# Attention: odd heads' softmax rows transposed into the two banks of other transposes, 13 steps behind the scores with a fourth row buffer

## The chip, the cores and the metric

The kernel runs on one core of a Trainium2 chip. The metric is device time in microseconds (us), the median of the runs shown. A profile records one execution: TensorE is PE in its rows (PEld for its weight loads), VectorE is DVE, ScalarE ACT, GpSimd POOL, and SyncE, which issues most transfers, SP. [...]

## The reference

Two layers of an encoder over 256 tokens of width 1024. Each layer is a half-step feed-forward block, two attention branches that share one projection, and another half-step feed-forward block:

```
x = x + 0.5 * swiglu(rms_norm(x, ffn1_norm), ...)
z = rms_norm(x, mix_norm) @ w_in          # na q|k|v, sw q, sw k|v, two gates
o_na = neighbourhood_attention(qa, ka, va, na_rpb)     # 8 heads of 64
o_sw = sliding_window_gqa(qs, ks_, vs, t5_bias, sink)  # 8 heads of 64, 2 key heads
merged = g[0] * (o_na @ w_branch_na) + g[1] * (o_sw @ w_branch_sw)
x = x + merged @ w_out
x = x + 0.5 * swiglu(rms_norm(x, ffn2_norm), ...)
```

Queries and keys are normalized for each head; scores get a bias (a learned one by relative position), and the sliding-window branch has a sink logit in its softmax. All is 32-bit floating point.

## The kernel before

**Precision.** Every large product is three products of halves. A value is split into a high and a low part (`split_to`, L181: ScalarE copies the high part, L182, and VectorE subtracts it, L183), and `three` (L167) issues high x high (L168), high x low (L169) and low x high (L170). A step below is one such triple of 128 x 512 matmuls.

**Order.** TensorE's order is that in which the code issues. A counter `now` advances by one with each step (`tick`), and `defer(lag, key, fn)` puts a piece of work into a list that `tick` empties when its time has come; `need(key)` calls it at once where its result is wanted. So the lags, counted in steps, say where in the stream of projection steps a piece of attention stands. The orders of ScalarE, VectorE, GpSimd and SP are laid out by a scheduler from the same program when it is built; each engine then takes its own queue in order.

**Attention.** `mix` runs the projection (w_in, in 512-column pieces), and between its steps the 16 heads, first the eight of the sliding-window branch (sw), then the eight of the neighbourhood branch (na). One head goes through these stages (`attend`, L520):

- `front` (L533): four score matmuls into a bank of tag sc (L547), bias and row maximum on VectorE into a row buffer S (L550), exponentials and sums on ScalarE (L553), the reciprocal on VectorE (L559), and the scaling of the rows on GpSimd (L560). S has LAG = 3 buffers.
- `turn` (L564), P_LAG = 10 steps later: four transposes of S into the one bank of tag pt (L568); ScalarE copies the high part ph out of it, and VectorE computes the low part pl, which reads pt too. Until pl is done the bank is taken.
- `back` (L575), V_LAG = 7.5 steps after that: four matmuls with v into po (L582), which ScalarE and VectorE combine into o (L586, L587); after every second head o is split into oB (sw) or oA (na).

**Other users of PSUM.** Projections and gates use two banks of tag g. Two banks of tag tp take the transposes of queries (L491) and keys (L508), of the merged branches (L707), of the normalized input (L199) and of the feed-forward block (L314). The low part of the keys, kl (L511), reads them, and the values va are read out of the g banks (L517, L518).

**Merge.** Behind the projection, `local` multiplies oB and `grid` oA with the branch weights. `grid` takes eight steps into banks br: k = 0, 1, 2 for both halves of the tokens, then k = 3 for both. The step k uses heads 2k and 2k + 1 of na, so k = 3 needs oA of heads 6 and 7. Weight pieces pass through a ring: a load into raw (4 buffers), ScalarE's wh and VectorE's wl (6 buffers each). The piece behind the branch weights is the first of w_out.

## Time and profile before

| what | value |
|---|---|
| median of 3 runs | 1088.5 us (1087.56 to 1088.72) |
| the profiled execution's own time | 1088.83 us |
| its span, first to last instruction | 1087.1 us |
| TensorE / VectorE / ScalarE / GpSimd busy | 1075.3 / 854.8 / 659.3 / 116.4 us |
| DMA: moved, mean rate | 212.63 MB, 196 GB/s |
| the attention stages | about 205 to 345 and 742 to 882 us |

A row of the timeline has its start, its length, the engine, the line, the operation with output and inputs, and in brackets how long the engine sat idle before it and what released it. Matmuls are pipelined, so one row's length reaches into the next; the distance of starts says how fast TensorE advances. A wait with several conditions is put down to the one that came last by the profile.

### The profile page before, as it was taken

How to read it: one execution, taken by the hardware profiler on the slowest of the kernel's cores; microseconds unless marked ns; L12 is line 12 of the kernel's file. 1: busy time of each engine (PE TensorE's matmuls, PEld its weight loads, DVE VectorE, ACT ScalarE, POOL GpSimd, SP SyncE). 2: the span in 40 equal slices, each digit the busy share in tenths (PEclk: the TensorE clock that was granted, in tenths of full speed). 3: DMA queues.
4: the chain of work that ended last, by engine and by line, in shares of the span. 5: the costliest groups of instructions: out<-in, count | busy, mean ns of one | idle time of the engine just before them, and what ended most of it. 6: DMA issues, size and time to landing. Idle time of an engine off the chain costs nothing.

```text
span 1087.1 us, 14699 instructions
## 1 busy us (share of the span) xinstructions
PE 1075.3 (99%) x5137; PEld 891.5 (82%) x5137; DVE 854.8 (79%) x1298; ACT 659.3 (61%) x1002; POOL 116.4 (11%) x118
## 2 busy tenths in 40 slices
PE   9999999999999999999999999999999999999998
PEld 6888888888888888888878888888888888888887
DVE  6888788889886778778877777888888767878785
ACT  6665654788764556565465656457877645656542
POOL 1400000243510000000000000003534000000000
PEclk9999999999999999999999999999999999999999
DMA  7876665755654676666657766547566555776652
GB/s 243 265 218 211 196 200 174 238 186 151 193 179 136 199 227 207 210 203 203 194 174 222 223 211 204 177 155 241 178 188 187 171 169 162 222 241 196 211 167 94
DMA packets 98828, 212.63 MB, mean 196 GB/s; under 512 B 7569, under 2 KB 13745, under 8 KB 98753
## 3 DMA queue, kind: packets, MB, share of 16 engines
q1 hardware_dynamic: 98560, 211.60, 62.3%
q8 instruction: 40, 0.66, 0.2%
q14 instruction: 36, 0.29, 0.1%
q0 software_dynamic: 192, 0.08, 0.1%
HBM read 210.59 MB, written 1.06 MB: 195 GB/s over the span
## 4 chain that ended last, share of the span: by engine, by line
PE 85%; DVE 8%; ACT 3%; issue 3%; DMA 1%; POOL 0%; ACTq 0%; DVEq 0%
PE g L168 19%; PE g L170 19%; PE g L169 18%; PE acc L168 6%; PE acc L170 6%; PE acc L169 6%; DVE wl L183 3%; PE tp L314 2%; ACT wh L182 1%; PE tp L169 1%; PE tp L170 1%; PE tp L168 1%; DMA raw<-in_w_d 1%; PE pt L568 1%; PE sc L547 1%
## 5 line engine op out<-in xcount | busy, mean ns | idle before, releaser
L183 DVE TENSOR_TENSOR wl<-raw,wh 128x1024 fp32r<-128x1024 f32 (+1 forms) x340 | 408.0, 1215 | 75.6 <-ACT wh L182 74.5
L182 ACT ACTIVATE wh<-raw 128x1024 fp32r<-128x1024 f32 (+1 forms) x340 | 348.8, 1044 | 117.4 <-PE g L170 39.3
L168 PE MATMUL g<-wh,xh 128*128 128x512 f32 (+1 forms) x976 | 386.1, 396 | 0.0
L170 PE MATMUL g<-wh,xl 128*128 128x512 f32 (+1 forms) x976 | 378.2, 387 | 0.7 <-DVE xl L183 0.7
L169 PE MATMUL g<-wl,xh 128*128 128x512 f32 (+1 forms) x976 | 377.9, 387 | 0.8 <-DVE wl L183 0.8
L170 PEld LDWEIGHTS g<-wh,xl 128*128 128x128 f32 x976 | 183.4, 188 | 40.8 <-DVE xl L183 2.1
L169 PEld LDWEIGHTS g<-wl,xh 128*128 128x128 f32 x976 | 183.9, 188 | 33.8 <-DVE wl L183 1.6
L168 PEld LDWEIGHTS g<-wh,xh 128*128 128x128 f32 x976 | 183.6, 188 | 32.5 <-DVE hh L445 0.2
L443 ACT ACTIVATE sg<-g,rs_y 128x256 f32<-128x256 f32 x88 | 41.2, 468 | 102.9 <-PE g L170 102.6
L342 DVE TENSOR_TENSOR u<-raw 128x512 f32<-128x512 f32 x56 | 38.5, 690 | 64.5 <-DMA raw<-in_w_d 64.1
L168 PE MATMUL acc<-wh,hi 128*128 128x512 f32 x200 | 78.9, 394 | 0.0
L170 PE MATMUL acc<-wh,lo 128*128 128x512 f32 x200 | 77.9, 390 | 0.0
L169 PE MATMUL acc<-wl,hi 128*128 128x512 f32 x200 | 77.9, 390 | 0.0
L174 POOL TENSOR_TENSOR rs_y<-ms,mhalf 128x1 f32<-128x1 f32 x12 | 6.6, 554 | 657.3 <-DVE ms L220 648.9
L445 DVE SCALAR_TENSOR_TENSOR hh<-g,rs_y,sg 128x256 f32<-128x256 f32 x88 | 42.2, 479 | 28.8 <-ACT sg L443 28.8
L182 ACT ACTIVATE corner<-raw 128x512 fp32r<-128x512 f32 x28 | 17.6, 629 | 62.3 <-DMA raw<-in_w_d 47.0
L560 POOL TENSOR_TENSOR S<-S,sm 128x512 f32<-128x512 f32 x32 | 37.1, 1159 | 71.5 <-DVE sm L559 45.4
L170 PEld LDWEIGHTS acc<-wh,lo 128*128 128x128 f32 x200 | 37.6, 188 | 8.0
L168 PEld LDWEIGHTS acc<-wh,hi 128*128 128x128 f32 x200 | 37.6, 188 | 7.5
L169 PEld LDWEIGHTS acc<-wl,hi 128*128 128x128 f32 x200 | 37.6, 188 | 7.5
L553 ACT ACTIVATE S<-S,mx 128x256 f32<-128x256 f32 x64 | 31.8, 498 | 7.5 <-DVE mx L550 7.4
L174 POOL TENSOR_TENSOR rs_y<-hv,mhalf 128x8 f32<-128x8 f32 (+1 forms) x16 | 27.0, 1693 | 31.4 <-DVE hv L476 28.4
(190 smaller groups left out, 1462.9 us busy)
## 6 DMA issues: line engine op xcount, KB each, us to landing
raw<-in_w_gu SPq DMA_DIRECT2D x176, 512.0 KB, 4.4
raw<-in_w_d SPq DMA_DIRECT2D x100, 512.0 KB, 4.4
raw<-in_w_in SPq DMA_DIRECT2D x64, 512.0 KB, 4.5
raw<-in_w_out SPq DMA_DIRECT2D x16, 512.0 KB, 3.5
bb<-in_b_gate SPq DMA_DIRECT2D x16, 256.0 KB, 3.4
raw<-in_w_bsw SPq DMA_DIRECT2D x8, 512.0 KB, 3.7
raw<-in_w_bna SPq DMA_DIRECT2D x8, 512.0 KB, 3.6
raw<-in_w_d SPq DMA_DIRECT2D x12, 256.0 KB, 2.6
```

Source lines behind the costliest of these rows:

```text
L168: nc.tensor.matmul(ps, xh, wh, start=first, stop=False)
L169: nc.tensor.matmul(ps, xh, wl, start=False, stop=False)
L170: nc.tensor.matmul(ps, xl, wh, start=False, stop=last)
L174: rstd_done[0] = nc.gpsimd.tensor_tensor(y, v, mhalf[:, :n], ALU.pow)
L182: linked("act", lambda: nc.scalar.activation(hi, src, AF.Copy))
L183: linked("dve", lambda: nc.vector.tensor_tensor(lo, src, hi.bitcast(F32), ALU.subtract))
L314: nc.tensor.transpose(tp[:, SLOT[t][i], :], hh[t][:, i * P:(i + 1) * P], ident)
L342: sub = lambda to, x, y: nc.vector.tensor_tensor(to, x, y, ALU.subtract)
L443: nc.scalar.activation(sg, ps[:, :FC], AF.Silu, scale=rstd[t])
L445: nc.vector.scalar_tensor_tensor(hh, ps[:, FC:], rstd[t], sg, op0=ALU.mult, op1=ALU.mult)
L553: nc.scalar.activation(S_[:, t, :], S_[:, t, :], AF.Exp, bias=mx[:, t:t + 1], scale=-1.0, accum_out=sm[:, t:t + 1])
L560: nc.gpsimd.tensor_tensor(S_, S_, sm.unsqueeze(2).to_broadcast([P, T, S]), ALU.mult)
```

## The change

Three edits. `turn` takes a bank of tag tp, of which there are two, for odd heads; of the sw branch (where sink_l is set) only from head 3 on. Even heads, and head 1 of sw, still use the one pt bank. P_LAG goes from 10 to 13, so each turn, and `back` behind it, stands three steps later in TensorE's order. LAG goes from 3 to 4, a fourth buffer S.

```diff
-LAG = 3
-H_LAG, NORM_LAG, QK_LAG, P_LAG, V_LAG, M_LAG = 7.9, 4.0, 16, 10, 7.5, 5.5
+LAG = 4
+H_LAG, NORM_LAG, QK_LAG, P_LAG, V_LAG, M_LAG = 7.9, 4.0, 16, 13, 7.5, 5.5
@@
                 @urgent
                 def turn(h, S_):
-                    tp = ps_acc.tile([P, T, T, P], F32, name="pt", tag="pt")
+                    if h % 2 and (sink_l is None or h > 1):
+                        tp = ps_tp.tile([P, T, T, P], F32, name="pt", tag="tp")
+                    else:
+                        tp = ps_acc.tile([P, T, T, P], F32, name="pt", tag="pt")
```

The lines behind it in the file are numbered three higher in the changed kernel (L568 becomes L571, L582 L585, L587 L590, L693 L696). Three places in the first layer follow; the second layer reads alike. The numbers in the names are those of buffers, and the brackets name the engines for whose signals an instruction waits.

TensorE at the transposes of na head 4, before:

```order
L582 MATMUL po_3156<-ph_3071,va_1815 128x256 [waits Activation_49]
L582 MATMUL po_3156<-pl_3072,va_1815 128x256
L582 MATMUL po_3156<-ph_3071,va_1815 128x256
L582 MATMUL po_3156<-pl_3072,va_1815 128x256
L568 MATMUL pt_3164<-ident_85,S_3039 128x128 [waits DVE_49,PE_49,Pool_49]
L568 MATMUL pt_3164<-ident_85,S_3039 128x128 x3
```

The same place in the changed program:

```order
L585 MATMUL po_3179<-ph_3099,va_1815 128x256 [waits DVE_49,Activation_49]
L585 MATMUL po_3179<-pl_3100,va_1815 128x256 [waits DVE_49]
L585 MATMUL po_3179<-ph_3099,va_1815 128x256
L585 MATMUL po_3179<-pl_3100,va_1815 128x256
L571 MATMUL pt_3187<-ident_85,S_3039 128x128 [waits PE_49,Pool_49]
L571 MATMUL pt_3187<-ident_85,S_3039 128x128 x3
```

The product ahead of it is now that of head 2, not of head 1, and the transposes no longer wait for VectorE.

TensorE in the merge, from behind the products of na head 7 (po, whose four rows stand directly ahead of this piece) to the seventh br step, before:

```order
L168 MATMUL br_3363<-wh_3352,oA_1817 128x512
L169 MATMUL br_3363<-wl_3353,oA_1817 128x512
L170 MATMUL br_3363<-wh_3352,oA_1817 128x512
L168 MATMUL br_3363<-wh_3352,oA_1817 128x512
L169 MATMUL br_3363<-wl_3353,oA_1817 128x512
L170 MATMUL br_3363<-wh_3352,oA_1817 128x512
L168 MATMUL br_3363<-wh_3358,oA_1817 128x512
L169 MATMUL br_3363<-wl_3359,oA_1817 128x512
L170 MATMUL br_3363<-wh_3358,oA_1817 128x512
L168 MATMUL br_3362<-wh_3358,oA_1817 128x512 [waits Activation_49]
L169 MATMUL br_3362<-wl_3359,oA_1817 128x512
L170 MATMUL br_3362<-wh_3358,oA_1817 128x512 [waits DVE_49]
```

And now, from the sixth br step to the seventh, with the products of na head 7 between them:

```order
L168 MATMUL br_3355<-wh_3350,oA_1817 128x512
L169 MATMUL br_3355<-wl_3351,oA_1817 128x512
L170 MATMUL br_3355<-wh_3350,oA_1817 128x512
L585 MATMUL po_3359<-ph_3331,va_1815 128x256 [waits DVE_49]
L585 MATMUL po_3359<-pl_3332,va_1815 128x256
L585 MATMUL po_3359<-ph_3331,va_1815 128x256
L585 MATMUL po_3359<-pl_3332,va_1815 128x256
L168 MATMUL br_3354<-wh_3350,oA_1817 128x512 [waits Activation_49]
L169 MATMUL br_3354<-wl_3351,oA_1817 128x512
L170 MATMUL br_3354<-wh_3350,oA_1817 128x512 [waits DVE_49]
```

The products of head 7 moved behind the three br steps that followed them, so that the step that reads their result (k = 3, first half of the tokens) stands right behind them.

VectorE in the same place, before (wl_3499 is the low part of the first w_out piece; the two rows o are those of na heads 6 and 7):

```order
L587 TENSOR_TENSOR o_3336<-o_3336,po_3335 64x256 [waits Activation_49]
L693 SCALAR_TENSOR_TENSOR gate1_1819<-gate1_1819,g_3328 128x512 [waits PE_49]
L183 TENSOR_TENSOR wl_3463<-raw_3460,wh_3462 128x1024 [waits DMAHW7_49,Activation_49]
L587 TENSOR_TENSOR o_3336<-o_3336,po_3335 64x256 [waits Activation_49]
L183 TENSOR_TENSOR oA_1817<-o_3336,oA_1817 128x256 [waits Activation_49]
L183 TENSOR_TENSOR wl_3499<-raw_3496,wh_3498 128x1024 [waits DMAHW0_49,Activation_49]
```

And now:

```order
L696 SCALAR_TENSOR_TENSOR gate1_1819<-gate1_1819,g_3319 128x512 [waits PE_49]
L183 TENSOR_TENSOR wl_3463<-raw_3460,wh_3462 128x1024 [waits DMAHW7_49,Activation_49]
L590 TENSOR_TENSOR o_3360<-o_3360,po_3359 64x256 [waits Activation_49]
L183 TENSOR_TENSOR wl_3499<-raw_3496,wh_3498 128x1024 [waits DMAHW0_49,Activation_49]
L590 TENSOR_TENSOR o_3360<-o_3360,po_3359 64x256 [waits Activation_49]
L183 TENSOR_TENSOR oA_1817<-o_3360,oA_1817 128x256 [waits Activation_49]
```

The low part of the w_out piece moved ahead of head 7's o. On ScalarE its high part moved likewise, ahead of that head's o.

## The prediction

> **What bounds the kernel now.** The page's busy table and its row of granted clock come first.

> ```profile
> PE 1075.3 (99%) x5137; PEld 891.5 (82%) x5137; DVE 854.8 (79%) x1298; ACT 659.3 (61%) x1002; POOL 116.4 (11%) x118
> PEclk9999999999999999999999999999999999999999
> ```

> TensorE is busy for 1075.3 of 1087.1 us at full clock, in an order fixed by hand. The change neither adds nor removes a matmul, so only TensorE's waits can change. I therefore read the busy time of the two attention stages (one for each layer), and of the two stretches in which TensorE waits longest there. Columns: stretch, length, PE, PEld, DVE, ACT and POOL busy (instructions), clock, DMA share, GB/s.

> ```profile
> 205.00:345.00 140.00, 137.82 (x753) 117.05 (x751) 117.61 (x230) 102.00 (x202) 45.59 (x37) 1.00 0.61 185
> 742.00:882.00 140.00, 137.85 (x752) 117.04 (x751) 117.87 (x230) 102.14 (x202) 45.32 (x37) 1.00 0.62 186
> 245.00:262.00 17.00, 16.14 (x91) 13.56 (x91) 15.96 (x37) 13.57 (x32) 7.26 (x7) 1.00 0.62 172
> 278.00:304.00 26.00, 24.96 (x137) 21.11 (x136) 22.65 (x47) 20.02 (x44) 12.50 (x10) 1.00 0.60 176
> ```

> TensorE idles 2.18 us in the first stage and 2.15 us in the second: no more than some 4.3 us can be won. VectorE is nearly full (15.96 of 17 us) where TensorE waits. The timeline, TensorE and VectorE, shows both waits of layer 0 and their twins:

> ```profile
> 259.05 0.39 PE L170 MATMUL g<-wh,xl 128*128 128x512 f32 x1
> 260.30 0.63 PE L568 MATMUL pt<-ident,S 128*128 128x128 f32 x4 [0.86 <-DVE pl L183]
> 301.87 0.28 PE L582 MATMUL po<-pl,va 128*128 128x256 f32 x1
> 303.18 0.63 PE L568 MATMUL pt<-ident,S 128*128 128x128 f32 x4 [1.03 <-DVE sm L559]
> 797.77 0.63 PE L568 MATMUL pt<-ident,S 128*128 128x128 f32 x4 [0.85 <-DVE pl L183]
> 840.61 0.63 PE L568 MATMUL pt<-ident,S 128*128 128x128 f32 x4 [1.01 <-DVE sm L559]
> 259.47 0.68 DVE L183 TENSOR_TENSOR pl<-pt,ph 128x512 fp32r<-128x512 f32 x1
> 302.36 0.68 DVE L183 TENSOR_TENSOR pl<-pt,ph 128x512 fp32r<-128x512 f32 x1
> 256.31 0.61 ACT L182 ACTIVATE ph<-pt 128x512 fp32r<-128x512 f32 x1
> ```

> Counted by these transposes, 260.30 is head 4 of the sliding-window branch (sw) and 303.18 head 4 of the neighbourhood branch (na). Both start right after the previous head's pl: 259.47 + 0.68 = 260.15, then 0.15 to the start; 302.36 + 0.68 = 303.04, then 0.14. So the wait is for the single pt bank, also where the row names another VectorE instruction that ended last (sm). The copy ph was done at 256.92, so pl itself stood 2.55 us in VectorE's queue.

> **The two waits go.** Both are even heads that wait for an odd one. With odd heads in the tp banks, head 4 shares its bank with head 2, a whole head earlier. The matmuls that read the late pl come later: in the new order po of sw 3 stands eight projection steps behind pt of head 3, and so does po of na 3: over 8 x 0.69 = 5.5 us, where pl ended 260.15 - 255.14 = 5.0 us behind its pt before (the pt row stands in the next part). Each wait's worth is start to start less the undisturbed spacing. The rows of the last term below give that spacing: 0.12 us after a 256-column matmul (324.74 to 324.86), and three steps of three 512-column matmuls in 2.06 us (324.86 to 326.92), so 0.69 for a step and 0.23 for a matmul. Thus 260.30 - 259.05 - 0.23 = 1.02 and 303.18 - 301.87 - 0.12 = 1.19, so 2.2 us for a layer, **4.4 us** for two (the idle times alone, 0.86 + 1.03 + 0.85 + 1.01, give 3.75: the lower bound).

> **What the moved steps do at the front.** Every pt stands three steps (2.1 us) later behind its scores. What VectorE has queued is the same work with two 0.4 us instructions (o and oB) fewer ahead of the second half of v:

> ```profile
> 255.14 0.60 PE L568 MATMUL pt<-ident,S 128*128 128x128 f32 x4
> 256.61 1.40 DVE L511 SCALAR_TENSOR_TENSOR kl<-tp,qkg,kh 128x512 fp32r<-128x512 f32 x2
> 257.93 0.41 DVE L183 TENSOR_TENSOR oB<-o,oB 128x256 fp32r<-128x256 f32 x1
> 259.07 0.48 DVE L518 SCALAR_TENSOR_TENSOR va<-g,rs_y,va 128x256 fp32r<-128x256 f32 x1
> 261.46 0.39 PE L168 MATMUL g<-wh,xh 128*128 128x512 f32 x1
> 250.73 1.99 DVE L183 TENSOR_TENSOR wl<-raw,wh 128x1024 fp32r<-128x1024 f32 x1
> ```

> That va releases the projection bank into which the matmul at 261.46 writes. Only pt of head 4 and one step lie between 260.30 and it, so this pt takes 261.46 - 260.30 - 0.69 = 0.47; in the new order it stands behind. Without it and without the wait the matmul comes at 261.46 - 1.02 - 0.47 = 260.0; va ends at 259.55 - 0.8 = 258.8: slack 1.2 us. Odd head 3 newly needs the tp bank of the last key transposes, which the first half of kl releases. In the new order pl of head 2 (0.60) and an o (0.4) stand behind kl instead of ahead: about 257.3 - 1.0 = 256.3, against pt of head 3 at 255.14 + 3 x 0.69 + 4 x 0.12 for one score group = 257.7. I take both at nothing; VectorE's doubled times (1.99 us, against 1.2 elsewhere, with GpSimd at work) can eat most of that, so their upper end is the whole present backlog less the slack, 2.55 - 1.2 = 1.4 us for a layer. A loss below nothing is excluded, as these are waits. Behind them TensorE's whole queue would stand.

> Of SP's queue, one b_gate load in each layer moves behind one more weight load. This is its row in the page's table of DMA issues, with the time to landing last:

> ```profile
> bb<-in_b_gate SPq DMA_DIRECT2D x16, 256.0 KB, 3.4
> ```

> A gate's projection ends eight steps (8 x 0.69 = 5.5 us) after that of the gate before, which frees the buffer; with 3.4 us for the load 2 us are left. I take nothing; if that cover were gone, a gate's bank would come free late, as in rival 3. GpSimd scales the same rows in the same order and gains 2.1 us; a fourth row buffer only lets scores start, and no score matmul waited for a row.

> **What becomes late next: the last head.** Three steps later there means into the merge. Its consumer does not move: the seventh of eight br steps (k = 3), which reads oA of na heads 6 and 7. Before, po of head 7 stood three br steps ahead of it; now it stands directly ahead. These are the rows of before:

> ```profile
> 324.74 0.28 PE L582 MATMUL po<-pl,va 128*128 128x256 f32 x1
> 324.86 0.40 PE L168 MATMUL br<-wh,oA 128*128 128x512 f32 x1
> 325.06 0.38 ACT L586 ACTIVATE o<-po 64x256 f32<-64x256 f32 x1 [1.47 <-DVE wl L183]
> 325.46 0.42 DVE L587 TENSOR_TENSOR o<-o,po 64x256 f32<-64x256 f32 x1 [0.42 <-ACT o L586]
> 325.92 0.42 ACT L182 ACTIVATE oA<-o 128x256 fp32r<-128x256 f32 x1 [0.49 <-DVE o L587]
> 326.37 0.43 DVE L183 TENSOR_TENSOR oA<-o,oA 128x256 fp32r<-128x256 f32 x1 [0.48 <-ACT oA L182]
> 321.76 1.23 DVE L183 TENSOR_TENSOR wl<-raw,wh 128x1024 fp32r<-128x1024 f32 x1 [0.85 <-ACT wh L182]
> 322.90 0.41 DVE L587 TENSOR_TENSOR o<-o,po 64x256 f32<-64x256 f32 x1
> 326.02 0.39 PE L170 MATMUL br<-wh,oA 128*128 128x512 f32 x1
> 326.49 1.06 ACT L182 ACTIVATE wh<-raw 128x1024 fp32r<-128x1024 f32 x1 [0.15 <-PE br L170]
> 326.92 0.39 PE L168 MATMUL br<-wh,oA 128*128 128x512 f32 x1
> 327.59 1.23 DVE L183 TENSOR_TENSOR wl<-raw,wh 128x1024 fp32r<-128x1024 f32 x1 [0.79 <-ACT wh L182]
> ```

> From the last po to the end of oA's high part: 325.92 + 0.42 - 324.74 = 1.60 us. At 326.92 it had been ready for 0.58 us: no wait. In the new order, with s the start of the sixth br step, the last of four po starts at s + 0.69 + 3 x 0.12 = s + 1.05 and the seventh step would start at s + 1.16. Its weight load would start one matmul (0.23) ahead, at s + 0.93. oA would be ready at s + 1.05 + 1.60 = s + 2.65.

> But the first w_out piece now stands ahead of this chain on ScalarE and VectorE (wh and wl were behind it). Its wh waits for the fifth br step, whose last matmul starts at s - 0.23: by 326.49 - 326.02 = 0.47 it starts at s + 0.24 and ends at s + 1.30, early enough for ScalarE's o at s + 1.37. Its wl starts 1.10 later than wh, at s + 1.34, and holds VectorE for 1.14 (the wl at 321.76 and the o behind it at 322.90); so VectorE's o starts at s + 2.48 instead of s + 1.77. Then 325.92 - 325.46 = 0.46 to ScalarE's oA, and 0.42: s + 3.36.

> What such a wait costs TensorE, layer 1's first projection shows, which waits for a stationary operand:

> ```profile
> 553.15 0.39 PE L169 MATMUL g<-wl,xh 128*128 128x512 f32 x1
> 553.46 0.68 DVE L183 TENSOR_TENSOR xl<-xg,xh 128x512 fp32r<-128x512 f32 x1
> 554.20 0.50 PE L170 MATMUL g<-wh,xl 128*128 128x512 f32 x1 [0.66 <-DVE xl L183]
> 554.53 0.39 PE L168 MATMUL g<-wh,xh 128*128 128x512 f32 x1
> ```

> Undisturbed, 554.53 would have been 553.15 + 0.46 = 553.61: lost 0.92. A weight load normally starts with the matmul ahead of its own, here at about 553.16; xl ended at 554.14, 0.98 later. So the loss is the lateness less 0.06: 3.36 - 0.93 - 0.06 = 2.37 us; with some 0.05 for oA's low part, 2.4 us for a layer, **4.8 us** for two. Bounds: 1.66 if that wl did not delay the chain (2.65 - 0.93 - 0.06), 2.5 if both low parts come late. No later work takes it up, as TensorE never idles behind it in the rows of before.

> **Sum.** -4.4 + 4.8 = +0.4 us. The profiled execution took 1088.83 (span 1087.1 and 1.73 around it), so 1089.2; the median of the runs is 0.33 lower, 1088.5, so **1088.9**. Bounds of the terms: -4.4 + 3.3 = -1.1 to -3.75 + 5.0 = +1.25, or 1087.4 to 1089.8.

> **Rivals.** (1) Forecast, a new wait as long as those removed: 0.64. (2) The chain from the last po costs TensorE less than its parts: faster from a wait under 1.1 us for a layer, down to 1084.1 without any. For it speaks that no br step waits now; against it, that four dependent instructions of 0.4 us follow po itself: 0.11. (3) Slower: the full VectorE queue at the front turns into a new wait for va's bank or kl's, from the point where va ends more than 1.2 us later than worked out. At 1.4 us for a layer that gives 1088.9 + 2.8 = 1091.7. For it: 15.96 of 17 us busy; against, less work ahead: 0.16. (4) The waits don't go (po then waits for the same pl): 1088.9 + 4.4 = 1093.3; against it speaks the distance worked out above: 0.06. (5) TensorE's clock falls after the long wait: 0.03. At the start of the program five matmuls take from 1.66 to 3.96:

> ```profile
> 1.66 2.50 PE L118 MATMUL idle<-blank 128*128 128x512 f32 x5 [1.66 <-DVE blank L113]
> 3.96 1.05 PE L199 MATMUL tp<-ident,x 128*128 128x128 f32 x4
> ```

> That is 0.46 each, twice the 0.23 above, though the clock row shows full speed. A slow stretch as long as these two rows (1.66 to 5.01) behind each wait would cost half its length, 1.7 us for a layer: 1092.3. Against it: after waits of 1.0 to 1.2 us the matmuls keep their pace. [...]

> **How the numbers follow.** What a measurement of this kernel can tell from no change is about 0.2%, 2.2 us. (2) is faster: 0.11. (1) is within it: 0.64. (3), (4) and (5) are slower: 0.25 together. The range reaches from the forecast's lower bound, with 0.6 us for what the walk leaves out, 1086.8, to (3) at 1092.0.

> **What would show it.** Right: no row of pt with an idle of 0.8 us or more; the seventh br step (L168) or its weight load waiting about 2.4 us for ScalarE's oA, in both layers, with a wl between ScalarE's and VectorE's o. Wrong: that wait under 1.6 us, or missing; a wait at a projection's first matmul or at a pt for kl; a clock under 1.0 behind the merge.

## The result: slower, with two waits that the prediction did not have

The changed kernel takes 1098.6 us (median of 4 runs, 1096.92 to 1099.25), against 1088.6 us (1087.56 to 1089.89) for the kernel before on the same chip: a ratio of 1.0087, 95% interval 1.0071 to 1.0103. It is slower by 10 us, where 1088.9 was forecast and 1092.0 was the upper end of the range. The profiled execution took 1099.25 us, its span 1097.5. Two executions of kernels below (1122.8 and 1805.6 us) ran throughout at a lower clock, 0.93 and 0.56 in the mean, and are left out of their medians and ratios.

First the page's busy row of the changed kernel:

```profile
PE 1080.3 (98%) x5137; PEld 894.6 (82%) x5137; DVE 860.8 (78%) x1298; ACT 658.3 (60%) x1002; POOL 119.8 (11%) x118
```

Then the view of its waits on TensorE (engine, output and line, releaser; us in total, times, the longest):

```profile
PE po L585 <- DVE o L590: 5.5, 4, 1.6
PE br L168 <- ACT oA L182: 4.3, 2, 2.2
```

Two things are to be seen. The waits of pt have gone from the list, as predicted, and br waits for oA, as predicted. But po waits for o, four times and for longer in all, and that stands nowhere in the prediction. And TensorE is busy for 5 us more with the same 5137 matmuls, so some of them were slow. The timeline has the new waits, each with the row ahead of it (TensorE, both layers):

```profile
268.95 0.39 PE L170 MATMUL g<-wh,xl 128*128 128x512 f32 x1
270.71 0.39 PE L585 MATMUL po<-ph,sv 128*128 128x256 f32 x1 [1.37 <-DVE o L590]
...
316.14 0.40 PE L170 MATMUL g<-wh,oB 128*128 128x512 f32 x1
318.09 0.39 PE L585 MATMUL po<-ph,va 128*128 128x256 f32 x1 [1.55 <-DVE o L590]
...
328.19 0.28 PE L585 MATMUL po<-pl,va 128*128 128x256 f32 x1
330.63 0.50 PE L168 MATMUL br<-wh,oA 128*128 128x512 f32 x1 [2.17 <-ACT oA L182]
...
811.76 0.39 PE L170 MATMUL g<-wh,xl 128*128 128x512 f32 x1
813.15 0.38 PE L585 MATMUL po<-ph,sv 128*128 128x256 f32 x1 [1.00 <-DVE o L590]
...
858.59 0.40 PE L170 MATMUL g<-wh,oB 128*128 128x512 f32 x1
860.54 0.39 PE L585 MATMUL po<-ph,va 128*128 128x256 f32 x1 [1.56 <-DVE o L590]
...
870.67 0.28 PE L585 MATMUL po<-pl,va 128*128 128x256 f32 x1
873.11 0.50 PE L168 MATMUL br<-wh,oA 128*128 128x512 f32 x1 [2.16 <-ACT oA L182]
```

Start to start, less the undisturbed 0.23 or 0.12 us, po lost 1.53, 1.72, 1.16 and 1.72 (6.1 us), and br 2.32 twice (4.6 us). Counted by their places, the po are those of sw head 4 and na head 5.

Behind the wait for oA the matmuls change their pace:

```profile
330.97 0.50 PE L169 MATMUL br<-wl,oA 128*128 128x512 f32 x1
331.27 0.63 PE L170 MATMUL br<-wh,oA 128*128 128x512 f32 x1
331.69 0.63 PE L168 MATMUL br<-wh,oA 128*128 128x512 f32 x1
...
334.25 0.52 PE L168 MATMUL g<-wh,oB 128*128 128x512 f32 x1
334.61 0.40 PE L169 MATMUL g<-wl,oB 128*128 128x512 f32 x1
334.85 0.39 PE L170 MATMUL g<-wh,oB 128*128 128x512 f32 x1
```

From 331.27 they start 0.43 us apart, and from 334.61 again 0.23. The eleven spacings from the start at 330.63 to that at 334.85 took 4.22 us instead of 11 x 0.23 = 2.53; some 0.1 of the difference lies in the first spacing (0.34 us; behind the wait at 554.20 of before, at full clock, it is 0.33), so 1.6 us is lost. The windows view of that stretch and of its twin has the granted clock third from the end:

```profile
330.60:334.60 4.00, 3.97 (x10) 3.10 (x11) 3.02 (x6) 1.06 (x1) 0.00 (x0) 0.57 0.41 131
873.00:877.00 4.00, 3.89 (x11) 2.95 (x12) 2.61 (x5) 1.12 (x2) 0.00 (x0) 0.60 0.41 131
```

So the account of the changed kernel is: -4.4 (pt) + 6.1 (po) + 4.6 (oA) + 3.2 (clock) = +9.5 us, against 1099.25 - 1088.83 = 10.4 between the profiled executions. The rest has no row of its own: from the first transposes of sw queries to the last br matmul the two stages take 135.85 and 135.24 us instead of 130.05 and 129.99, which is 11.0 us, so 1.5 us of spacings lengthened by some 0.2 us and less come on top within the stages, and 0.6 us are won back outside them.

What the po waited for is on VectorE's queue (at the end with two rows of ScalarE, the o and oA of head 7):

```profile
266.36 3.18 DVE L183 TENSOR_TENSOR wl<-raw,wh 128x1024 fp32r<-128x1024 f32 x2
269.46 0.74 DVE L637 SCALAR_TENSOR_TENSOR gate<-g,rs_y,bb 128x512 f32<-128x512 f32 x1
270.23 0.42 DVE L590 TENSOR_TENSOR o<-o,po 64x256 f32<-64x256 f32 x1
...
315.36 2.35 DVE L183 TENSOR_TENSOR wl<-raw,wh 128x1024 fp32r<-128x1024 f32 x2
317.63 0.40 DVE L590 TENSOR_TENSOR o<-o,po 64x256 f32<-64x256 f32 x1
...
328.45 1.23 DVE L183 TENSOR_TENSOR wl<-raw,wh 128x1024 fp32r<-128x1024 f32 x1 [1.89 <-ACT wh L182]
329.71 0.42 DVE L590 TENSOR_TENSOR o<-o,po 64x256 f32<-64x256 f32 x1
...
328.51 0.38 ACT L589 ACTIVATE o<-po 64x256 f32<-64x256 f32 x1
330.17 0.42 ACT L182 ACTIVATE oA<-o 128x256 fp32r<-128x256 f32 x1 [1.28 <-DVE o L590]
```

In the first two places the o of the head before (sw 3, na 4) stands behind two weight pieces: ScalarE's half of it was done at 268.15 and 315.94, VectorE's began 2.1 and 1.7 us later. In the third a wl stands between ScalarE's and VectorE's o of head 7, as predicted. All po share one bank, and in the program every po matmul waits until VectorE's o of the preceding head is done: that of the pair before, which is plain, but also that of the even head in the same pair, which lies in the other half of the bank.

### The profile page after: what moved, and what is told of

Same layout as the page of the kernel before. It is cut to its first block, busy times and chain, and to the rows that moved or that the text cites. A ratio compares the mean times of both kernels' runs of the same rounds, so it can differ in the third digit from the quotient of the medians.

```text
span 1097.5 us, 14679 instructions
## 1 busy us (share of the span) xinstructions
PE 1080.3 (98%) x5137; PEld 894.6 (82%) x5137; DVE 860.8 (78%) x1298; ACT 658.3 (60%) x1002; POOL 119.8 (11%) x118
## 3 DMA queue, kind: packets, MB, share of 16 engines
HBM read 210.59 MB, written 1.06 MB: 193 GB/s over the span
## 4 chain that ended last, share of the span: by engine, by line
PE 89%; DVE 6%; ACT 2%; issue 2%; DMA 0%; DVEq 0%; ACTq 0%
PE g L168 20%; PE g L170 19%; PE g L169 19%; PE acc L170 6%; PE acc L168 6%; PE acc L169 6%; DVE wl L183 3%; PE tp L314 2%; ACT wh L182 1%; PE tp L168 1%; PE tp L170 1%; PE tp L169 1%; PE po L585 1%; PE sc L547 1%; PE g L235 1%
## 5 line engine op out<-in xcount | busy, mean ns | idle before, releaser
L183 DVE TENSOR_TENSOR wl<-raw,wh 128x1024 fp32r<-128x1024 f32 (+1 forms) x340 | 411.8, 1228 | 71.9 <-ACT wh L182 70.4
L182 ACT ACTIVATE wh<-raw 128x1024 fp32r<-128x1024 f32 (+1 forms) x340 | 348.4, 1043 | 119.8 <-PE g L170 40.4
L168 PE MATMUL g<-wh,xh 128*128 128x512 f32 (+1 forms) x976 | 386.3, 396 | 0.0
L170 PE MATMUL g<-wh,xl 128*128 128x512 f32 (+1 forms) x976 | 378.3, 388 | 0.7 <-DVE xl L183 0.7
L169 PE MATMUL g<-wl,xh 128*128 128x512 f32 (+1 forms) x976 | 377.9, 387 | 0.4 <-DVE wl L183 0.4
L170 PEld LDWEIGHTS g<-wh,xl 128*128 128x128 f32 x976 | 183.4, 188 | 40.9 <-DVE xl L183 2.1
L169 PEld LDWEIGHTS g<-wl,xh 128*128 128x128 f32 x976 | 183.8, 188 | 33.7 <-DVE wl L183 1.1
L168 PEld LDWEIGHTS g<-wh,xh 128*128 128x128 f32 x976 | 183.6, 188 | 32.8 <-DVE hh L445 0.2
L168 PE MATMUL acc<-wh,hi 128*128 128x512 f32 x200 | 78.9, 394 | 0.0
L170 PE MATMUL acc<-wh,lo 128*128 128x512 f32 x200 | 78.0, 390 | 0.0
L169 PE MATMUL acc<-wl,hi 128*128 128x512 f32 x200 | 77.9, 390 | 0.0
L182 ACT ACTIVATE corner<-raw 128x512 fp32r<-128x512 f32 x28 | 17.7, 630 | 64.4 <-DMA raw<-in_w_d 48.9
L560 POOL TENSOR_TENSOR S<-S,sm 128x512 f32<-128x512 f32 x32 | 40.5, 1267 | 61.6 <-DVE sm L559 42.3
L170 PEld LDWEIGHTS acc<-wh,lo 128*128 128x128 f32 x200 | 37.6, 188 | 8.0
L169 PEld LDWEIGHTS acc<-wl,hi 128*128 128x128 f32 x200 | 37.6, 188 | 7.5
L168 PEld LDWEIGHTS acc<-wh,hi 128*128 128x128 f32 x200 | 37.6, 188 | 7.5
## 6 DMA issues: line engine op xcount, KB each, us to landing
bb<-in_b_gate SPq DMA_DIRECT2D x16, 256.0 KB, 3.8
raw<-in_w_d SPq DMA_DIRECT2D x12, 256.0 KB, 2.6
```

The source lines that it names most:

```text
L168: nc.tensor.matmul(ps, xh, wh, start=first, stop=False)
L169: nc.tensor.matmul(ps, xh, wl, start=False, stop=False)
L170: nc.tensor.matmul(ps, xl, wh, start=False, stop=last)
L182: linked("act", lambda: nc.scalar.activation(hi, src, AF.Copy))
L183: linked("dve", lambda: nc.vector.tensor_tensor(lo, src, hi.bitcast(F32), ALU.subtract))
L560: nc.gpsimd.tensor_tensor(S_, S_, sm.unsqueeze(2).to_broadcast([P, T, S]), ALU.mult)
```

## The experiments

The first question was which of the edits costs what. Ratios are to the kernel before, with 95% intervals.

**The banks alone** (10 steps, three row buffers):

```diff
-LAG = 4
-H_LAG, NORM_LAG, QK_LAG, P_LAG, V_LAG, M_LAG = 7.9, 4.0, 16, 13, 7.5, 5.5
+LAG = 3
+H_LAG, NORM_LAG, QK_LAG, P_LAG, V_LAG, M_LAG = 7.9, 4.0, 16, 10, 7.5, 5.5
```

> Only the banks: odd heads' pt in the tp banks, rows still 10 steps behind their scores, three row buffers. Theory (the banks win the two pt waits of a layer, everything that was lost comes with the 13 steps): 1088.6 - 4.4 = 1084.2 us, no PE row of pt with an idle of 0.8 us or more, no wait of po for VectorE's o above 0.5 us, granted clock 1.00. Rival (the tp banks themselves upset VectorE's order, so that po waits for o): 1084.2 + 6 = about 1090 us with po waits of 1.0 to 1.6 us.

Measured: 1089.8 us, ratio 1.0017 (1.0008 to 1.0026). Neither the theory nor the rival holds: the time is near the rival's, but not for its reason. The waits for pl are gone and po does not wait, but another wait has come:

```profile
256.92 0.63 PE L571 MATMUL pt<-ident,S 128*128 128x128 f32 x4 [2.20 <-DVE kl L511]
...
794.44 0.83 PE L571 MATMUL pt<-ident,S 128*128 128x128 f32 x4 [2.20 <-DVE kl L511]
```

With 10 steps, sw head 3 asks for the tp bank of the last key transposes before VectorE has read it. The 2.2 us eat what the banks won, and in layer 1 the clock fell behind them too, by the windows view:

```profile
256.90:260.90 4.00, 3.98 (x24) 3.53 (x25) 3.50 (x11) 2.26 (x7) 0.48 (x2) 1.00 0.75 222
794.40:798.40 4.00, 3.96 (x15) 3.45 (x16) 3.04 (x10) 1.88 (x6) 0.13 (x1) 0.57 0.63 209
```

So the 13 steps were what made the tp banks usable for odd heads.

**The steps and row buffers alone** (pt of every head in one bank):

```diff
-                    if h % 2 and (sink_l is None or h > 1):
-                        tp = ps_tp.tile([P, T, T, P], F32, name="pt", tag="tp")
-                    else:
-                        tp = ps_acc.tile([P, T, T, P], F32, name="pt", tag="pt")
+                    tp = ps_acc.tile([P, T, T, P], F32, name="pt", tag="pt")
```

> Only the 13 steps and the fourth row buffer, pt of all heads in the one bank of before. In the changed kernel pt of head 4 starts after the previous head's pl has ended in both branches (261.80 against 260.52 + 0.68 = 261.20; 305.02 against 302.55 + 0.67 = 303.22), so theory: the lag alone already takes the pt waits away and the banks then buy nothing: 1098.6 us, within 1, with the same three waits of a layer (po twice, 1.0 to 1.6 us each; br for oA 2.2 us). Rival (the gain is the banks'): 1098.6 + 4.4 = 1103.0 us with pt waits of 0.8 us or more. Rival (the po waits come with the banks): 1098.6 - 6 + 4.4 = 1097, no po waits.

Measured: 1105.5 us, ratio 1.0158 (1.0144 to 1.0171), dearer than all three cases. The sw wait for pl has gone, as expected, but in na head 3 now comes so close behind head 2 that it waits longer than any before:

```profile
303.25 1.09 PE L568 MATMUL pt<-ident,S 128*128 128x128 f32 x4 [3.03 <-DVE pl L183]
```

The expectation had taken this pl for that of another head. The clock fell behind this wait and that for oA, in both layers (0.57 or 0.58 in the 4 us behind each). po waits for o in sw only (1.35 and 1.00 us). So with 13 steps the second bank does earn its keep, in na.

**The fourth row buffer alone** (kernel before, LAG = 4).

> The kernel before with a fourth row buffer and nothing else. Theory (a row buffer only lets scores start, and none waited for one): 1088.3 us, within 0.6. Rival (VectorE gets another order because the scheduler sees buffers free earlier, and po or br waits appear): 1090 us or more.

Measured: 1088.4 us, ratio 1.0001 (0.9992 to 1.0010). It costs and gains nothing.

**Head 7 of na at 10 steps again**, to price the end of the stage:

```diff
-                    defer(P_LAG, (name, h, 0), lambda: turn(h, S_))
+                    defer(10 if sink_l is None and h == 7 else P_LAG, (name, h, 0), lambda: turn(h, S_))
```

> The changed kernel, but na head 7 keeps 10 steps, so its po stands three br steps ahead of the seventh one again. Theory (the wait for oA costs 2.3 us and the slow clock behind it 1.55 us, in each layer): 1098.6 - 2 x 3.85 = 1090.9 us, granted clock 1.00 behind the merge, the two po waits unchanged. Rival (the slow matmuls have another cause at that place): only the wait goes, 1098.6 - 4.6 = 1094.0 us, matmuls still 0.43 us apart for some 3 us.

Measured: 1092.6 us, ratio 1.0043 (1.0029 to 1.0057). The wait for oA is gone and the slow stretch with it (clock 1.00 from 322 to 345). It is 1.7 us more than expected, and 1.1 of them are in one row of each layer: po of head 7, now closer behind head 6, waits for its o.

```profile
326.22 0.39 PE L585 MATMUL po<-ph,va 128*128 128x256 f32 x1 [0.57 <-DVE o L590]
```

**Filling the wait.** If idleness itself lowers the clock, work of no use should keep it up:

```diff
                 for ks in ((0, 1, 2), (3,)):
+                    if d == 0 and ks == (3,):
+                        for stage in range(2):
+                            need(("na", 6, stage), ("na", 7, stage))
+                        fill = ps_acc.tile([P, 512], F32, name="fill", tag="pt")
+                        for _ in range(8):
+                            nc.tensor.matmul(fill, oA[0][:, 0, 0, :], pieces[0][0][:, 0, :], start=True, stop=True)
```

> The changed kernel plus eight matmuls (the first w_bna row block by oA of heads 0 and 1, 512 columns each) into the idle pt bank between po of na head 7 and the seventh br step; nothing reads them. 8 x 0.23 = 1.84 us of the 2.17 us that TensorE idles there. Theory (the idle time itself lowers the clock): br starts no earlier, but the matmuls behind it are 0.23 us apart: 1098.6 - 2 x 1.55 = 1095.5 us, clock 1.00 in that stretch. Rival (another cause at that place, such as the transfers there): 1098.6 us, matmuls 0.43 us apart as before. If the eight matmuls delayed the chain to oA, over 1099.

Measured: 1095.9 us, ratio 1.0071 (1.0058 to 1.0083): with 1.84 us of useless matmuls in each layer its median is 2.8 us below that without them (1.7 us by the ratios). The timeline (TensorE, then ScalarE):

```profile
328.34 0.28 PE L585 MATMUL po<-pl,va 128*128 128x256 f32 x1
328.46 2.00 PE L722 MATMUL fill<-wh,oA 128*128 128x512 f32 x8
330.30 0.39 PE L168 MATMUL br<-wh,oA 128*128 128x512 f32 x1
...
329.52 0.42 ACT L182 ACTIVATE oA<-o 128x256 fp32r<-128x256 f32 x1 [0.49 <-DVE o L590]
```

And the windows view behind the fill:

```profile
330.30:334.30 4.00, 4.00 (x19) 3.34 (x18) 3.22 (x6) 2.12 (x2) 0.00 (x0) 1.00 0.08 9
```

The clock stays at 1.00, as the theory has it. But the transfers are fewer here too (DMA share 0.08, where the changed kernel had 0.41), so this run alone does not tell idle time from transfers; the last experiment does. It has another side effect: the fill reads branch weights, so the w_out piece had to wait for it and came behind the chain of head 7. oA was then done 329.94 - 328.34 = 1.60 us behind the last po, against 330.59 - 328.19 = 2.40 in the changed kernel. So br stands 1.96 us behind the last po instead of 2.44, and the 2.8 us are not the clock's alone. But it shows, by accident, what that wl adds to the chain: 0.8 us.

**Fewer steps**, 12 and 11 in place of 13:

> The changed kernel with 12 steps in place of 13: po of na head 7 stands one br step ahead of the seventh. Theory (the wait for oA shrinks by the 0.69 us of a step, and the clock only falls behind waits of about 2 us): wait 2.17 - 0.69 = 1.5 us, matmuls behind it 0.23 apart; so 2 x (0.69 + 1.55) = 4.5 us less than 1098.6 at the end of the stage, 1094.1 us if the two po waits stay as they are. Rival (the clock falls behind any wait over 1.2 us): 1098.6 - 1.4 = 1097.2 us.

> The changed kernel with 11 steps: po of na head 7 two br steps ahead of the seventh. Theory: wait for oA 2.17 - 1.38 = 0.8 us, clock 1.00; pt of sw head 3 stands one projection step and a score group further behind the key transposes than with the banks alone: its wait for kl 2.20 - 0.69 - 0.47 = 1.0 us. Without po waits 1088.4 - 4.4 + 2 x (0.8 + 1.0) = 1087.6 us; with the po waits of the changed kernel 1093.6 us. Rival (the po waits come only with 13 steps): the former.

Measured: 1092.9 us for 12 (1.0034, 1.0021 to 1.0047) and 1092.2 for 11 (1.0036, 1.0023 to 1.0049). Here are the waits of layer 0, first for 12, then for 11:

```profile
257.30 0.63 PE L571 MATMUL pt<-ident,S 128*128 128x128 f32 x4 [0.91 <-DVE kl L511]
327.42 0.50 PE L168 MATMUL br<-wh,oA 128*128 128x512 f32 x1 [2.19 <-ACT oA L182]
```
```profile
257.01 0.63 PE L571 MATMUL pt<-ident,S 128*128 128x128 f32 x4 [1.17 <-DVE kl L511]
327.52 0.50 PE L168 MATMUL br<-wh,oA 128*128 128x512 f32 x1 [0.81 <-ACT oA L182]
328.81 0.50 PE L170 MATMUL br<-wh,oA 128*128 128x512 f32 x1 [0.56 <-DVE oA L183]
```

With 12 steps the median came close to what was expected, for other reasons: the wait for oA did not shrink (2.19 us; the chain starts from the wl, not from po) and the clock fell (0.68), but the two long po waits are gone and a wait for kl has come. With 11 the wait for oA's high part is as expected (0.81), without a slow stretch, but oA's low part is late by another 0.56. The long po waits are gone, as the rival had it (four of at most 0.32 us are left); its 1087.6 is missed all the same, since the br matmuls lose 1.7 us a layer, start to start, and not 0.8. The wait for kl grows in layer 0 with each step taken back: none at 13, 0.91, 1.17, 2.20 us at 10 (in layer 1 it is 0.55 at 12 and 0.82 at 11).

**A second po bank, pt of all heads in the tp banks:**

```diff
-                    if h % 2 and (sink_l is None or h > 1):
-                        tp = ps_tp.tile([P, T, T, P], F32, name="pt", tag="tp")
-                    else:
-                        tp = ps_acc.tile([P, T, T, P], F32, name="pt", tag="pt")
+                    tp = ps_tp.tile([P, T, T, P], F32, name="pt", tag="tp")
...
-                        po[0] = ps_acc.tile([P, 2, T, P], F32, name="po", tag="po")
+                        po[0] = ps_acc.tile([P, 2, T, P], F32, name="po", tag="po", bufs=2)
```

(Left out: the other users of these tags, the bank of the first matmuls and those of the down projection, take the same two po banks.)

> The changed kernel (13 steps, four row buffers), but pt of all heads in the two tp banks, and the bank that pt had given to po as a second one. Theory (the two po waits of a layer are waits for the single po bank, released by VectorE's o of the odd head before): they go, 2 x (1.5 + 1.7) = 6.4 us less, 1092.2 us, with the br wait and the slow clock behind it unchanged. Rival (po waits for o only because VectorE is behind, and its late pl comes up next): 1096 to 1099 us, with waits of po for pl.

Measured: 1111.5 us, ratio 1.0206 (1.0184 to 1.0229). It failed as a fix, since the first heads of sw now wait for the banks of query and key transposes:

```profile
238.36 0.63 PE L568 MATMUL pt<-ident,S 128*128 128x128 f32 x4 [1.63 <-ACT qT L493]
257.20 0.99 PE L568 MATMUL pt<-ident,S 128*128 128x128 f32 x4 [3.74 <-DVE kl L511]
323.78 0.39 PE L582 MATMUL po<-ph,va 128*128 128x256 f32 x1 [1.57 <-DVE o L587]
```

Yet as a test it says something. The long po wait of sw is gone; that of na head 5 stays, because head 5 shares its bank with head 4 of the same pair. So a bank for each head was next.

**Odd heads' po in a bank of their own**, from the fourth head of sw on:

```diff
-                    if h % 2 and (sink_l is None or h > 1):
+                    if sink_l is None or h > 2:
...
+                    bank = po[0]
+                    if h % 2 and (sink_l is None or h > 2):
+                        bank = ps_acc.tile([P, 2, T, P], F32, name="pq", tag="pt")
...
```

(Left out: the matmuls write to `bank`, and o is read from it.)

> The changed kernel, but from the fourth head of sw on an odd head's po gets a bank of its own (the pt bank; the rows of these heads are transposed into the two tp banks, odd or even). Theory (each po waits for VectorE's o of the head before it, because all po lie in one bank, even the two halves of a pair): the two po waits of a layer go (1.5 + 1.7 us start to start, and some 0.2 of small ones), the br wait and the slow clock behind it stay: 1098.6 - 2 x 3.3 = 1092.0 us. Rival (VectorE is simply that late, and the next thing that po reads, pl, is late too): 1097 to 1099 us, with po waiting for pl at the same places. Rival (the even heads' pt in the tp banks find these taken): pt waits for kl or pl of 1 us or more.

Measured: 1096.9 us, ratio 1.0080 (1.0065 to 1.0095). No po waits for o any more. In sw the time is won. In na most of it is lost again one row later, where a branch step finds its bank not yet read by VectorE, which is behind by the same two pieces:

```profile
318.10 0.50 PE L168 MATMUL g<-wh,oB 128*128 128x512 f32 x1 [1.24 <-DVE gate L640]
```

So theory and rival both hold, each in one place: in sw freeing the bank takes the loss away; in na VectorE's lateness comes up again at the next bank, so freeing this one is not enough. Between the same two marks as above the two stages win 4.2 us together, of which 1.7 show in the median. By their intervals (1.0065 to 1.0095 against 1.0071 to 1.0103) this kernel can't be told from the changed one; that the bank matters is read from the rows, not from the time.

**All three waits taken away** (the last one, and head 7 at 10 steps):

> The same, and na head 7 keeps 10 steps. If the account of the changed kernel is complete (pt waits gone by 4.4 us; po waits 6.6, wait for oA 4.6 and slow clock 3.1 us added), all that was added goes: 1088.3 - 4.4 = 1083.9 us, the time of the version with even heads in the tp banks (1083.3), clock 1.00 and no wait over 0.6 us in the attention stages. Rival (13 steps cost something that the waits don't show): 1086 us or more.

Measured: 1087.7 us, ratio 0.9996 (0.9986 to 1.0006); the profiled execution took 1086.08 us, at clock 1.00. Of the 13.9 us added, 10.9 are back by the medians (1098.6 - 1087.7; 9.9 by the ratios). The theory's 1083.9 is not reached, and the rival's condition, 1086 us or more, is met. Against the version with even heads, which follows, the two stages take 129.36 and 128.78 us instead of 127.62 and 127.69: 2.8 us more, of which two waits for gate (0.79 and 0.58, as in the row above) are 1.7 start to start. The other 1.1 us, and the 1.6 us between the profiled execution and the median, stay open, so the account is shown to within these.

**Even heads in the tp banks instead**, with 10 steps and three row buffers (the condition is shown against the changed kernel):

```diff
-                    if h % 2 and (sink_l is None or h > 1):
+                    if h % 2 == 0 and (sink_l is None or h > 3):
```

> The banks alone put pt of sw head 3 behind the key transposes' bank, where it waited 2.20 us for VectorE's kl (256.92). Here the even heads take the tp banks instead of the odd ones (sw from head 4 on, na all), with 10 steps and three row buffers as before: head 4 still has another bank than head 3, and the first tp bank is asked for a head later, when kl is long done. Theory (each term of the banks as predicted, only the place was wrong): the two pt waits of a layer go and nothing comes: 1088.4 - 4.4 = 1084.0 us, no pt wait over 0.5 us, clock 1.00. Rival (a head's pt always finds VectorE behind, so the wait moves to po for the same pl): 1088 us, with po rows waiting 0.8 to 1.2 us for pl.

Measured: 1083.3 us, ratio 0.9953 (0.9940 to 0.9966), faster than both kernels. TensorE's order is that of before, and so is VectorE's but for 2 of 1298 instructions. The stages hold no wait over 0.3 us, and TensorE is busy throughout:

```profile
205.00:345.00 140.00, 139.71 (x760) 119.05 (x760) 117.75 (x231) 102.25 (x203) 46.34 (x37) 1.00 0.61 187
742.00:882.00 140.00, 139.72 (x755) 118.68 (x754) 116.72 (x230) 100.76 (x201) 45.66 (x37) 1.00 0.60 184
```

**How long may TensorE idle?** A program of its own, which leaves the computation out and has idle times instead, profiled once (shortened here):

```
for lap in range(14):
    for n in (512, 900, 1150, 1350, 1550, 1800, 2100, 2600):
        33 to 39 matmuls of 512 columns, the first with w as its weights
        vector: one element out of the last result; then w from n elements
```

> A program of its own, which leaves the whole computation out (the output is the input): 14 laps of eight stretches of 33 to 39 matmuls of 512 columns (7.6 to 9.0 us), and between any two a wait for two VectorE instructions, the second over 512 to 2600 elements, so idle times of about 1.0 to 3.6 us in a row of eight steps. Theory (the clock is set by how busy TensorE was in windows of some 3.4 us that run on by themselves): never slow behind waits under 1.6 us, always behind those over 3 us, sometimes in between, more often the longer the wait; each slow stretch about 3.4 us long, and the times at which slow stretches end differ by multiples of one period. Rival (a fixed limit for the length of the wait, counted from the last matmul): a sharp step between two lengths, and no common period.

Two of the waits, alike in length (timeline, TensorE):

```profile
309.09 0.50 PE L80 MATMUL ps<-a,w 128*128 128x512 f32 x1 [1.85 <-DVE w L85]
396.82 0.50 PE L80 MATMUL ps<-a,w 128*128 128x512 f32 x1 [1.85 <-DVE w L85]
```

And the 6.5 us behind each (windows view, without ScalarE, which does nothing here; clock third from the end):

```profile
309.09:315.59 6.50, 6.50 (x29) 5.38 (x30) 0.00 (x0) 0.00 (x0) 1.00 0.00 0
396.82:403.32 6.50, 6.50 (x21) 5.18 (x22) 0.00 (x0) 0.00 (x0) 0.74 0.00 0
```

No transfer runs in either (DMA share 0.00), so transfers did not lower the clock here. The trace of the changed kernel records both of its slow stretches with a granted clock of 0.50, for 3.413 us each. Taken at 0.50, a clock of 0.74 over 6.5 us is a slow stretch of 2 x 0.26 x 6.5 = 3.4 us, and whenever the clock fell here it was by about that (3.0 to 3.4). All 112 waits:

| idle time, us | 0.98 | 1.38 | 1.65 | 1.85 | 2.06 | 2.32 | 2.63 | 3.15 |
|---|---|---|---|---|---|---|---|---|
| waits | 14 | 14 | 14 | 14 | 14 | 14 | 14 | 14 |
| slow behind it | 0 | 0 | 0 | 7 | 3 | 4 | 9 | 13 |

## Why the prediction was wrong, step by step

- **"The two waits go"** (-4.4): right. No pt waits for pl in the changed kernel, and the version with even heads in the tp banks, in which nothing else changes, shows the size: 5.0 us between the medians.
- **"What the moved steps do at the front"** (0): right for va and for kl, none of which is waited for; with 10 steps instead of 13 kl costs 2.2 us a layer, so the 13 steps paid for that cover. VectorE's queue ahead of va was much as worked out there: va ended at 258.85, where 258.8 was expected. What this part did not look at is where the o of the heads would stand in that queue (below).
- **"What becomes late next: the last head"** (+4.8): right in place, cause and size. 2.32 us a layer instead of 2.4, with that wl between ScalarE's and VectorE's o, and the chain takes 2.40 us with the wl and 1.60 without.
- **The step that failed** is the one on po: "The matmuls that read the late pl come later." It asked only when po's operands are ready, not when its bank is free. In the new order po of sw 4 and of na 5 come before VectorE, whose o stands behind two weight pieces, has read out the head before. That cost 6.1 us, put at nothing in the prediction. No rival had it: (3) put VectorE's lateness at va's and kl's banks at the front, (4) at pl. Freeing the bank took the wait away in sw; in na VectorE's lateness came up in the next bank.
- **Rival (5)**, the clock, had a chance of 0.03, and happened: 1.6 us a layer, priced at 1.7. Against it I had put that waits up to 1.2 us left the pace alone, which is true (none of the 42 waits up to 1.65 us above was followed by a slow stretch) and does not decide: that one of 2.4 us would leave it alone too was my estimate, which no run had shown. In the runs above some 1.85 us within one window was enough, and the changed kernel's waits were 2.17 and 2.16. That both layers of the profiled execution lost it is in part luck: by the table, 7 of 28 waits of 2.06 and 2.32 us do. The mean clocks of the four runs say as much: 0.996 in those of 1099.25 and 1099.14 us, 0.998 in those of 1098.1 and 1096.92, which fits two slow stretches and one (a clock of 0.50 for 3.413 us is 0.16% of the span).

Of the 10 us above the forecast, 6.1 are thus po and 3.2 the clock.

## What to carry to other kernels

When steps are moved on the busiest engine, ask of each moved instruction two questions, not one: when are its operands ready, and who must have read out the bank that it writes, including the other half of that bank. Read VectorE's new order as well as TensorE's: here an o of 0.4 us behind two weight pieces came 2 us late. And look at the length of a wait on TensorE that cannot be avoided: in the program with idle times alone none of 42 waits up to 1.65 us was followed by a slow stretch, and 7 of 14 of 1.85 us were. Each slow stretch cost the changed kernel another 1.6 us; with 1.84 us of useless matmuls in the wait the clock stayed at 1.00.

## What the hardware showed that I had not expected

Of the 70 waits of 1.85 to 3.15 us in the program with idle times alone, 36 were followed by a slow stretch, and which ones was told by where they fell in a grid of windows of 3.413 us, not by their length alone. Of the 2.20 us waits for kl in the version with the banks alone, that of layer 1 was (clock 0.57 in the 4 us behind it) and that of layer 0 was not (1.00); so runs of the same program can differ by the 1.6 us that a slow stretch cost. The seven runs with 12 steps, which have such a wait in each layer (2.19 us in layer 0), fit that: 1090.17 and 1091.30 us at a mean clock of 0.999, 1092.11 at 0.998, 1092.93 to 1093.59 at 0.996 or 0.997.
